# The low parts of the projection weights on GpSimd, with later due times in the order of TensorE's work

## The chip, the cores and the metric

One Trainium2 chip, one core of it. The metric is the device time of one execution in microseconds (us), the median over several runs. PE is TensorE, DVE is VectorE, ACT is ScalarE, POOL is GpSimd, SP is SyncE, whose queue starts most of the DMAs.

## The reference

One layer of a trunk with T = 1024 frames and width 1024, in float32. The input is normalised per frame and projected to many pieces; three gated recurrences (HGRN2 with 4 heads, GLA with 4 heads, mLSTM with 4 heads) work on the pieces in chunks of frames; their normalised and gated outputs are joined and projected back.

```python
h = _rmsnorm(x, norm_w[l])
parts = _split_columns(h @ w_in[l] + b_in[l])
y_hg = _gated_head_norm(_hgrn2_branch(parts, lower_bounds[l]), parts["hg_z"], hg_norm_w[l])
y_gla = _gated_head_norm(_gla_branch(parts, gla_w_a2[l], gla_b_a2[l]), parts["gla_z"], gla_norm_w[l])
y_ml = _gated_head_norm(_mlstm_branch(parts, ml_conv_w[l], ml_conv_b[l]), parts["ml_z"], ml_norm_w[l])
y = jnp.concatenate([y_hg, y_gla, y_ml], axis=-1).astype(x.dtype)
x = x + y @ w_out[l]
...
return _rmsnorm(x, final_norm_w)
```

## The kernel before

**Products.** Every float32 product of the projections is made of three matmuls on parts in the rounded type fp32r. A weight tile of 128x1024 goes through three steps in `load_w`: SP starts its DMA to `wraw` (two buffers), ACT copies it to the high part `whi` (rounding, line 230), and DVE subtracts to get the low part `wlo` (line 231). `whi` and `wlo` have four buffers each. PE then adds high x high, high x low and low x high in PSUM.

**Stages.** `proj_first` makes the first three pieces of head 0 (`f0`, `q0`, `z0`) while the input arrives, the weights cut into column parts (`cuts`). In it `row_sums` sums squares per frame, POOL raises the means to -1/2 (line 268), `row_scale` spreads the result over the partitions by transposes (line 275) and ACT copies it to `RSB` (line 276). The first pieces then leave PSUM through multiplications by `RSB` on DVE (line 339). The three wide loads (840, 840 and 560 columns, `load_wide`) are the weights of `v0`. After that `projections` runs over all other pieces: `proj_nt` (lines 346 to 348) and the transposed forms `proj_tn` and `proj_tn2` (lines 379 to 381 and 398 to 400), whose results DVE takes out of PSUM in `scaled` (line 406). The last part multiplies by the output weights in seven products of half size; the sums that these need are made by DVE in `sum_steps` (line 1075) along the way.

**The order of the work.** PE's order is set by the class `Weave`, at the time when the program is written: the projections are the main stream, and chains (trees, states, outputs, gates) are put between its matmuls. A chain yields its own cost on PE, a lag after which it may go on, and, if it holds a PSUM slot, for how long (`yield cost, lag, slot, hold`). These are estimates in model us (`proj_nt` counts 0.65 for three matmuls); the numbers decide after which projection matmul a chain's matmuls stand. In `proj_first` the orders of PE, ACT and SP are those of the code. All other orders, those of DVE and POOL among them, come from the scheduler of the framework, which keeps a fence `tc.issue_after(ins)`: what is issued in the block stands behind `ins` on the engine of `ins`.

**Chains that the change touches.** `radix4` (from line 440) is the finest step of the trees of the four HGRN2 heads; its `slack` is 1.2 for head 0 and 0 for the others. `tail` (line 655) makes a head's states and starts its outputs. `gla_alpha` (line 747) makes the gates of GLA: two rounds of logits in the PSUM slots `po` (line 750), a subtraction on DVE (line 768) that reads them, and an exponential on ACT. `ml_chain` makes the mLSTM heads: `ml_states` (line 851 on PE, line 857 on DVE, which writes the states `S`) and `ml_out` (lines 871 and 879 on PE, the latter reading `S`). `norm_transposed` normalises an output: squares on ACT (line 558), mean and power on POOL (lines 216 and 217), scaling on ACT (line 561), transposes on PE (line 566).

Of the kernel before, what the change touches and what calls it, by code (L numbers as in the profile page):

```python
# [7 lines left out]
F32 = mybir.dt.float32  # L8
F32R = mybir.dt.float32r
U8 = mybir.dt.uint8  # L10
AF = mybir.ActivationFunctionType
# [125 lines left out]
def kernel(ctx: ExitStack, tc: tile.TileContext, x, xt, wt, wide, cols, vbias, wa2, wq, fw, masks, sel,  # L137
                      ident_in, out):
    nc = tc.nc
# [9 lines left out]
    po = ctx.enter_context(tc.tile_pool(name="po", bufs=2, space=PS))  # L149
# [10 lines left out]
    RSB = const.tile([128, T], F32, name="RSB")  # L160
# [56 lines left out]
        nc.gpsimd.tensor_tensor(dst, dst, mhalf[:, 0:dst.shape[1]], op=OP.pow)  # L217


    def load_w(src, cuts=None, raw=None, hilo=None):  # L220

        raw = wp.tile([128, 1024], F32, name="wraw", bufs=2) if raw is None else raw
        if hilo is None:
            hilo = [wp.tile([128, 1024], F32R, name=nm, bufs=4) for nm in ("whi", "wlo")]
        hi, lo = hilo

        def part(a, b):
            s = slice(a, b)
            nc.sync.dma_start(raw[:, s], src[:, s])
            nc.scalar.activation(hi[:, s], raw[:, s], AF.Copy)  # L230
            nc.vector.tensor_sub(lo[:, s], raw[:, s], hi[:, s].bitcast(F32))  # L231
        if cuts is None:
            part(0, src.shape[1])
            return hi, lo
        return (hi, lo), [lambda a=a, b=b: part(a, b) for a, b in zip(cuts, cuts[1:])]

# [34 lines left out]
    def row_scale():  # L271
        for half in range(2):
            p = ptr.tile([128, 512], F32, name="tp")
            for j in range(4):
                nc.tensor.transpose(p[:, j * 128:(j + 1) * 128], rs[:, 4 * half + j:4 * half + j + 1].to_broadcast([128, 128]), ident)
            nc.scalar.activation(RSB[:, 512 * half:512 * half + 512], p, AF.Copy)


    wide_w, scales, marks = [], [], []
# [6 lines left out]
    def proj_first(pieces):  # L286

        ws, loads = [], []
        for i in range(3):
            raw = fp.tile([128, 1024], F32, name="al", bufs=2) if i == 2 else None  # L290
            t, steps = load_w(wt[WIDX[pieces[i][0]]], WCUTS, raw)
            ws.append(t)
            loads.append(steps)
        ps = [[pl.tile([128, 512], F32, name=nm) for _ in range(2)] for pl, nm in ((pmain, "pm"), (po, "po"), (ptree, "pt"))]
        done = [0, 0, 0]

        def matmuls(i, k):
            hi, lo = ws[i]
            for kk in range(done[i], k):
                ks = slice(128 * kk, 128 * kk + 128)  # L300
                for half in range(2):
                    s = slice(512 * half, 512 * half + 512)
                    nc.tensor.matmul(ps[i][half], hi[:, ks], HI[kk][:, s], start=kk == 0, stop=False)
                    nc.tensor.matmul(ps[i][half], lo[:, ks], HI[kk][:, s], start=False, stop=False)
                    nc.tensor.matmul(ps[i][half], hi[:, ks], LO[kk][:, s], start=False, stop=kk == KC - 1)
            done[i] = k
        for k in range(KC):
            if k == 0:
                loads[0][0]()
            build_h(k, 2 if k < 2 else 1)  # L310
            if k == 0:
                loads[1][0]()
                loads[2][0]()
            for i in range(3):
                for a in range(1, len(WCUTS) - 1):
                    if (WORDER[i] + 2 * (a - 1)) == k:
                        loads[i][a]()
            if k >= 3:
                square(k - 3)
            if k < KOUT:  # L320
                for i in range(3):
                    matmuls(i, k + 1)
        for k in range(KC - 3, KC):
            square(k)
        load_wide(0, [fp.tile([128, 1024], F32R, name="al", bufs=2) for _ in range(2)])
        matmuls(0, KC)
        load_wide(1)
        matmuls(1, SUMS)
        mean = row_sums()
        matmuls(1, KC)  # L330
        load_wide(2)
        matmuls(2, SCALE)
        row_scale()
        matmuls(2, KC)
        with tc.issue_after(mean):
            load_consts()
        for (_, dst, evac), pp in zip(pieces, ps):
            for half in range(2):
                nc.vector.tensor_mul(dst(half), pp[half], RSB[:, 512 * half:512 * half + 512])
                evac(half)  # L340

    def nt_half(hi, lo, s):
        p = pmain.tile([128, 512], F32, name="pm")
# [97 lines left out]
    def radix4(Q, K, F, Kc, dA, l4, slack):  # L441

        g = 4 ** l4
        n = 128 // g
        Q4, K4, F4 = (a.rearrange("p (n j g) -> p n j g", j=4, g=g) for a in (Q, K, F))
        P = [F4[:, :, j, g - 1:g] for j in range(4)]
        over = lambda j0, j1: F4[:, :, j0:j1, g - 1:g].to_broadcast([128, n, j1 - j0, g])
        qm = wk.tile([128, 768], F32, name="qm")  # L450
        M = qm.rearrange("p (n j g) -> p n j g", j=6, g=g)
        nc.scalar.activation(qm.rearrange("p (n x) -> p n x", n=n)[:, :, 0:3 * g],
                             Q.rearrange("p (n x) -> p n x", n=n)[:, :, g:4 * g], AF.Copy)
        nc.vector.tensor_tensor(M[:, :, 3:5, :], Q4[:, :, 2:4, :], over(1, 3), op=OP.mult)
        marks.append(nc.vector.tensor_tensor(M[:, :, 5, :], M[:, :, 4, :], P[1].to_broadcast([128, n, g]), op=OP.mult).ins)
        yield 0.0, 4.0 + slack
        yield "pt"
        p = ptree.tile([128, 512], F32, name="pt")
        for c in range(4):
            for a in range(0, 128, 32):  # L460
                q = (4 * c + a // 32) * 48
                nc.tensor.matmul(p[a:a + 32, 48 * c:48 * c + 48], Kc[:, c, a:a + 32], qm[:, q:q + 48], start=True, stop=True)
        pm = p[:, 0:192].rearrange("p (m j g) -> p m j g", j=6, g=g)
        d4 = dA.rearrange("p c (m j g) -> p (c m) j g", j=4, g=g)
        for off, j, w in ((0, 0, 3), (96, 3, 2), (160, 5, 1)):
            mask = mk4[:, l4, off:off + 32 * w].rearrange("p (m j g) -> p m j g", j=w, g=g)
            nc.vector.copy_predicated(d4[:, :, 4 - w:4, :], mask, pm[:, :, j:j + w, :])
        nc.vector.tensor_tensor(Q4[:, :, 1, :], Q4[:, :, 1, :], P[0].to_broadcast([128, n, g]), op=OP.mult)
        nc.vector.tensor_tensor(Q4[:, :, 2:4, :], M[:, :, 3:6:2, :], P[0][:, :, None].to_broadcast([128, n, 2, g]), op=OP.mult)
        nc.vector.tensor_tensor(P[2], P[2], P[3], op=OP.mult)  # L470
        nc.vector.tensor_tensor(P[1], P[1], P[2], op=OP.mult)
        nc.vector.tensor_tensor(K4[:, :, 0:3, :], K4[:, :, 0:3, :], over(1, 4), op=OP.mult)
        marks.append(nc.vector.tensor_tensor(P[3], P[0], P[1], op=OP.mult).ins)
        yield 0.7, 1.9 + slack, "pt", 3.0 + slack

    def tree(Q, K, F, A, dA, nh, half, done, slack=0.0):

# [171 lines left out]
    def tail(w, heads, rows, Q, K, F, V, zs, yi, trees, ready, out_done):  # L649

        yield lambda: ready() and 0 in trees
        S = wk.tile([128, NC, 130], F32, name="S", bufs=1)
        Kc = K.rearrange("p (c t) -> p c t", c=NC)
        states_done, first = [], []
        for half in range(2):
            yield lambda: half in trees
            yield from states(Kc, V[0], F, list(zip(heads, rows)), S, half)
            yield 0.0, 2.2
            states_done.append(half)
            if len(heads) > 1:  # L660
                w.start(pair_out(att, Q, V[0], S, zs, yi, half, states_done, first, out_done))
                continue
            for i, h in enumerate(heads):
                yield lambda: len(zs) > i
                w.start(att_out(h, att[:, (yi + i) % 2], Q[:, i], V[0], S, zs[i], yi + i, half, states_done, first, out_done))
# [77 lines left out]
    def gla_alpha(r, als):  # L743
# [21 lines left out]
        with tc.issue_after(marks[-1]):  # L765
            for half in range(2):
                s = slice(512 * half, 512 * half + 512)
                nc.vector.tensor_sub(al[:, s], ps[half], al[:, s])
        for half in range(2):
            yield 0.0, 0.0, "po", 2.0 + half  # L770
        nc.scalar.activation(al, al, AF.Exp, scale=1.0 / 16.0)
        als.append(al)

# [123 lines left out]
    def ml_chain(w, r, ready, PQK, Vs, ogs, gates, ys, zs, done):  # L897
# [22 lines left out]
        yield lambda: len(gates) == NC  # L920
        yield from ml_states(r, K, E, V, S, 1)
        states_of.append(r)
        yield from ml_out(r, Q, S, V, ogs[0], ys, 1, gates)
        for h in range(2):
            yield lambda: len(zs) > h
            for half in range(2):
                s = slice(512 * half, 512 * half + 512)
                dst = y_tile(4 + h)[:, 1] if r else ys[h]
# [263 lines left out]
    with tc.manual_schedule(engines={mybir.EngineType.PE}):  # L1192
# [87 lines left out]
        for c in range(4):  # L1280
            parts = [R] if c < 3 else [slice(512, 896), last]
            for n, cols in enumerate(parts):
                pc_ = slice(cols.start - 512, cols.stop - 512)
                p = ptree.tile([128, 512], F32, name="pt") if n else pa[c]
# [93 lines left out]
```

## Time and profile before

| what | value |
|---|---|
| median of 3 runs | 756.55 us (756.28 to 756.6) |
| the profiled execution, its own time | 757.12 us |
| its span in the trace | 755.3 us |
| busy: PE, DVE, ACT, POOL | 740.4, 471.6, 353.2, 60.2 us |

The span runs from the first to the last instruction in the trace; 1.8 us of the profiled execution lie outside it. Busy times count what an engine works on instructions; a matmul's weight load (PEld) overlaps the matmul before it. Rows of the trace have the start, the duration, the engine, the line of the code, the operation, the tiles and their sizes, and, in brackets, how long the engine stood idle before and whose end released it.

### The profile page before, as it was taken

The numbers are of one execution on the slowest core, as the hardware profiler recorded it, in microseconds if no ns is written. First come the engines' busy times: TensorE is split into PE (matmuls) and PEld (weight loads), VectorE is DVE, ScalarE is ACT, GpSimd is POOL, SyncE is SP. The second block draws the span as 40 slices with busy tenths as digits, with TensorE's granted clock in tenths as the row PEclk, the third lists the DMA queues.
The fourth block names the chain that finished last, engine by engine and source line by source line (L and its number), as shares of the span: only waits on it lengthen the run. The fifth ranks groups of instructions, "written<-read, shape, count | busy, mean of one in ns | idle before, by whom it ended". The sixth has DMA issues, their size and how long they took to land.

```text
span 755.3 us, 13831 instructions
## 1 busy us (share of the span) xinstructions
PE 740.4 (98%) x5550; PEld 619.6 (82%) x5550; DVE 471.6 (62%) x1004; ACT 353.2 (47%) x772; POOL 60.2 (8%) x107
## 2 busy tenths in 40 slices
PE   9999998999999999999999999999999999999996
PEld 7888886899887899788988878878877878888886
DVE  6987767766467538523662384353564358899864
ACT  6661577842343431544044553345270556454543
POOL 2000130010010020012001200101000110000011
PEclk9999999999999999999999999999999999999998
DMA  8443652332542232102020120031210077543323
GB/s 307 137 154 115 189 183 75 110 91 88 196 146 92 88 137 85 51 29 84 31 85 29 55 84 1 2 126 69 71 56 0 18 252 275 167 139 112 87 109 140
DMA packets 30545, 80.58 MB, mean 107 GB/s; under 512 B 3648, under 2 KB 7232, under 8 KB 30480
## 3 DMA queue, kind: packets, MB, share of 16 engines
q1 hardware_dynamic: 29664, 78.89, 31.3%
q8 instruction: 44, 0.72, 0.4%
q0 software_dynamic: 672, 0.53, 0.3%
q10 hardware_dynamic: 144, 0.26, 0.1%
q14 instruction: 21, 0.17, 0.1%
HBM read 63.74 MB, written 15.93 MB: 105 GB/s over the span
## 4 chain that ended last, share of the span: by engine, by line
PE 77%; ACT 7%; DVE 6%; DMA 6%; issue 1%; SPq 1%; POOL 0%; POOLq 0%; DVEq 0%; ACTq 0%
PE pm L346 10%; PE pm L348 10%; PE pm L347 9%; PE pm L398 4%; PE pm L379 4%; PE pm L400 4%; PE pm L399 4%; PE pm L380 3%; PE pm L381 3%; DMA wraw<-in_wt_dram 3%; DMA wraw<-in_wq_dram 2%; PE pm L1157 2%; PE pm L1158 2%; PE pm L1156 2%; DVE wlo L231 2%
## 5 line engine op out<-in xcount | busy, mean ns | idle before, releaser
L346 PE MATMUL pm<-hT,whi 128*128 128x512 f32 x400 | 163.5, 409 | 0.0
L348 PE MATMUL pm<-hT,wlo 128*128 128x512 f32 x400 | 156.8, 392 | 0.0
L347 PE MATMUL pm<-hT,whi 128*128 128x512 f32 x400 | 156.8, 392 | 0.0
L346 PEld LDWEIGHTS pm<-hT,whi 128*128 128x128 f32 x400 | 75.5, 189 | 16.9 <-issue 1.5
L348 PEld LDWEIGHTS pm<-hT,wlo 128*128 128x128 f32 x400 | 75.5, 189 | 16.7
L347 PEld LDWEIGHTS pm<-hT,whi 128*128 128x128 f32 x400 | 75.8, 189 | 13.6
L230 ACT ACTIVATE whi<-wraw 128x1024 fp32r<-128x1024 f32 (+4 forms) x47 | 45.7, 974 | 78.9 <-PE pm L347 31.7
L379 PE MATMUL pm<-whi,hT 128*128 128x256 f32 (+1 forms) x232 | 67.9, 293 | 0.0
L380 PE MATMUL pm<-wlo,hT 128*128 128x256 f32 (+1 forms) x232 | 66.0, 285 | 0.0
L381 PE MATMUL pm<-whi,hT 128*128 128x256 f32 (+1 forms) x232 | 66.0, 284 | 0.0
L231 DVE TENSOR_TENSOR wlo<-wraw,whi 128x1024 fp32r<-128x1024 f32 (+4 forms) x47 | 52.5, 1120 | 20.3 <-ACT whi L230 19.9
L406 DVE SCALAR_TENSOR_TENSOR big<-pm,rs,vb 128x256 f32<-128x256 f32 x72 | 30.9, 456 | 44.1 <-PE pm L400 27.3
L398 PE MATMUL pm<-whi,hT 128*128 128x512 f32 x128 | 52.5, 410 | 0.0
L400 PE MATMUL pm<-whi,hT 128*128 128x512 f32 x128 | 50.1, 392 | 0.0
L399 PE MATMUL pm<-wlo,hT 128*128 128x512 f32 x128 | 49.9, 390 | 0.0
L379 PEld LDWEIGHTS pm<-whi,hT 128*128 128x128 f32 x232 | 44.2, 190 | 0.8
L380 PEld LDWEIGHTS pm<-wlo,hT 128*128 128x128 f32 x232 | 44.3, 191 | 0.1
L381 PEld LDWEIGHTS pm<-whi,hT 128*128 128x128 f32 x232 | 44.2, 191 | 0.0
L533 ACT ACTIVATE att<-dc 32x128 f32<-32x128 f32 (+1 forms) x48 | 16.5, 343 | 54.8 <-DVE dc L513 54.3
L358 DVE TENSOR_TENSOR zg<-pm,RSB 128x512 f32<-128x512 f32 x22 | 15.2, 691 | 31.8 <-PE pm L348 26.7
L398 PEld LDWEIGHTS pm<-whi,hT 128*128 128x128 f32 x128 | 24.0, 188 | 7.7 <-issue 1.8
L400 PEld LDWEIGHTS pm<-whi,hT 128*128 128x128 f32 x128 | 24.0, 188 | 5.4
(391 smaller groups left out, 1502.4 us busy)
## 6 DMA issues: line engine op xcount, KB each, us to landing
wraw<-in_wt_dram SPq DMA_DIRECT2D x39, 512.0 KB, 3.8
wraw<-in_wq_dram SPq DMA_DIRECT2D x27, 512.0 KB, 3.6
wraw<-wsum SPq DMA_DIRECT2D x18, 512.0 KB, 3.5
wsum<-wraw SPq DMA_DIRECT2D x12, 512.0 KB, 2.9
big<-ydram SPq DMA_DIRECT2D x18, 256.0 KB, 5.4
ydram<-zg SPq DMA_DIRECT2D x8, 256.5 KB, 2.4
big<-in_xt_dram SPq DMA_DIRECT2D x4, 512.0 KB, 5.5
ydram<-zg SPq DMA_DIRECT2D x8, 255.5 KB, 2.6
```

The source lines that it names most:

```text
L230: nc.scalar.activation(hi[:, s], raw[:, s], AF.Copy)
L231: nc.vector.tensor_sub(lo[:, s], raw[:, s], hi[:, s].bitcast(F32))
L346: nc.tensor.matmul(p, hi[:, ks], HI[k][:, s], start=k == 0, stop=False)
L347: nc.tensor.matmul(p, hi[:, ks], LO[k][:, s], start=False, stop=False)
L348: nc.tensor.matmul(p, lo[:, ks], HI[k][:, s], start=False, stop=k == KC - 1)
L379: nc.tensor.matmul(p, HI[k][:, ts], hi[:, ks], start=k == 0, stop=False)
L380: nc.tensor.matmul(p, HI[k][:, ts], lo[:, ks], start=False, stop=False)
L381: nc.tensor.matmul(p, LO[k][:, ts], hi[:, ks], start=False, stop=k == KC - 1)
L398: nc.tensor.matmul(p, HI[k][:, ts], hi[:, ks], start=k == 0, stop=False)
L399: nc.tensor.matmul(p, HI[k][:, ts], lo[:, ks], start=False, stop=False)
L400: nc.tensor.matmul(p, LO[k][:, ts], hi[:, ks], start=False, stop=k == KC - 1)
L406: nc.vector.scalar_tensor_tensor(dst, p, rs[:, c:c + 1], b, op0=OP.mult, op1=OP.add)
```

## The change

The low part of a weight tile goes from DVE to POOL where the tile is loaded whole: 39 tiles of 128x1024 and the three wide ones. The cut tiles of `proj_first` and the tiles of the output product stay on DVE. The whole loads that follow `proj_first` are fenced behind ACT's second copy to `RSB` and behind the last multiplication of the evacuation (which is on DVE). Four due times in the order of PE's work are made later: radix4's lag and slot (by `slack`), the lag of `tail`, the slots of `gla_alpha`'s logits, and a new lag in `ml_chain` ahead of the second `ml_out`.

```diff
+    evacuated = []
...
-            nc.vector.tensor_sub(lo[:, s], raw[:, s], hi[:, s].bitcast(F32))
+            (nc.vector if cuts else nc.gpsimd).tensor_sub(lo[:, s], raw[:, s], hi[:, s].bitcast(F32))
         if cuts is None:
-            part(0, src.shape[1])
+            with ExitStack() as fences:
+                for ins in evacuated:
+                    fences.enter_context(tc.issue_after(ins))
+                part(0, src.shape[1])
...
-            nc.scalar.activation(RSB[:, 512 * half:512 * half + 512], p, AF.Copy)
+            copy = nc.scalar.activation(RSB[:, 512 * half:512 * half + 512], p, AF.Copy)
+        return copy.ins
...
-        row_scale()
+        scale = row_scale()
...
-                nc.vector.tensor_mul(dst(half), pp[half], RSB[:, 512 * half:512 * half + 512])
+                mul = nc.vector.tensor_mul(dst(half), pp[half], RSB[:, 512 * half:512 * half + 512])
                 evac(half)
+        evacuated.extend((scale, mul.ins))
...
-        yield 0.7, 1.9 + slack, "pt", 3.0 + slack
+        yield 0.7, 1.9 + 2.0 * slack, "pt", 3.0 + 2.0 * slack
...
-            yield 0.0, 2.2
+            yield 0.0, 3.2
             states_done.append(half)
...
-            yield 0.0, 0.0, "po", 2.0 + half
+            yield 0.0, 0.0, "po", 6.0 + half
...
         states_of.append(r)
+        yield 0.0, 3.5
         yield from ml_out(r, Q, S, V, ogs[0], ys, 1, gates)
```

After the change the lines below these places have numbers that are 2 to 8 higher (line 231 is 233, line 276 is 281, line 879 is 886).

ACT at the end of `proj_first`, before: the third wide tile, the first whole tile of the projections, then the copies to `RSB` and the sigmoid of `f0`.

```order
L230 ACTIVATE whi<-wraw 128x560
L230 ACTIVATE whi<-wraw 128x1024
L276 ACTIVATE RSB<-tp 128x512 x2
L950 ACT_TABLE_LOAD
L950 ACTIVATE f<-f,pc 128x512 x2
```

The same place with the change:

```order
L232 ACTIVATE whi<-wraw 128x560
L281 ACTIVATE RSB<-tp 128x512 x2
L232 ACTIVATE whi<-wraw 128x1024
L958 ACT_TABLE_LOAD
L958 ACTIVATE f<-f,pc 128x512 x2
```

The copies to `RSB` stand ahead of the first whole tile now.

POOL around the power of the row scale, before: the mask, the power, then copies for the gates.

```order
L175 AFFINE_SELECT neg<-neg 128x128
L268 TENSOR_TENSOR rs<-rs,mhalf 128x8
L432 COPY zg<-zg 128x1
L683 COPY big<-big 128x8x8
L685 COPY big<-big 128x8x16
```

With the change:

```order
L175 AFFINE_SELECT neg<-neg 128x128
L233 TENSOR_TENSOR al<-wraw,al 128x840
L233 TENSOR_TENSOR wlo<-wraw,whi 128x840
L273 TENSOR_TENSOR rs<-rs,mhalf 128x8
L233 TENSOR_TENSOR wlo<-wraw,whi 128x560
L233 TENSOR_TENSOR wlo<-wraw,whi 128x1024
L439 COPY zg<-zg 128x1
```

Two wide low parts stand ahead of the power, and one wide and the first whole one behind it.

PE in the second half of mLSTM (heads 0 and 1), before: the states, then at once the outputs, among projection matmuls.

```order
L348 MATMUL pm<-hT,wlo 128x512
L851 MATMUL pt<-big,kd 64x129 x6
L871 MATMUL po<-big,att 128x129 x4
L879 MATMUL po<-S,big 128x129 x4
L346 MATMUL pm<-hT,whi 128x512
```

With the change, the states:

```order
L858 MATMUL pt<-big,kd 64x129 x6
L353 MATMUL pm<-hT,whi 128x512
L354 MATMUL pm<-hT,whi 128x512
L355 MATMUL pm<-hT,wlo 128x512
```

and the outputs further on:

```order
L355 MATMUL pm<-hT,wlo 128x512
L878 MATMUL po<-big,att 128x129 x4
L886 MATMUL po<-S,big 128x129 x4
```

Between the two there are 18 projection matmuls now; before there were none.

## Rows read from the trace of the kernel before

**Rows 1.** The page: busy time, share of the span and instructions of each engine.

```profile
PE 740.4 (98%) x5550; PEld 619.6 (82%) x5550; DVE 471.6 (62%) x1004; ACT 353.2 (47%) x772; POOL 60.2 (8%) x107
```

**Rows 2.** PE's waits: who waited, for whom; us in all, how often, the longest.

```profile
PE po L879 <- DVE S L857: 2.2, 2, 1.2
PE po L750 <- DVE al L768: 1.6, 1, 1.6
PE pm L379 <- DVE f L339: 1.5, 1, 1.5
...
PE pm L379 <- DVE big L406: 0.9, 2, 0.7
PE pt L462 <- DVE f L470: 0.5, 1, 0.5
PE pt L592 <- ACT kd L575: 0.4, 1, 0.4
PE po L640 <- DVE S L598: 0.4, 1, 0.4
```

**Rows 3.** Timeline of the first evacuation: start us, us, engine, line, operation.

```profile
40.93 1.06 ACT L276 ACTIVATE RSB<-tp 128x512 f32<-128x512 f32 x2
...
41.06 1.22 DVE L231 TENSOR_TENSOR wlo<-wraw,whi 128x1024 fp32r<-128x1024 f32 x1 [1.66 <-ACT whi L230]
...
42.20 0.68 DVE L339 TENSOR_TENSOR f<-pm,RSB 128x512 f32<-128x512 f32 x1
...
42.94 0.40 PE L379 MATMUL pm<-al,hT 128*128 128x280 f32 x1 [1.53 <-DVE f L339]
```

**Rows 4.** Window after L750's wait: busy PE, PEld, DVE, ACT, POOL, granted clock, DMA.

```profile
126.00:131.00 5.00, 5.00 (x45) 3.89 (x46) 2.33 (x9) 4.90 (x10) 0.00 (x0) 0.66 0.01 3
```

**Rows 5.** Groups by line and shape: busy us, mean ns, then idle before.

```profile
L231 DVE TENSOR_TENSOR wlo<-wraw,whi 128x1024 fp32r<-128x1024 f32 x39 | 47.7, 1226 | 19.9 <-ACT whi L230 19.5
...
L685 POOL COPY big<-big 128x128 f32<-128x128 f32 x1 | 0.4, 435 | 0.0
...
L683 POOL COPY big<-big 128x64 f32<-128x64 f32 x1 | 0.3, 307 | 23.6 <-DVE big L406 23.6
```

**Rows 6.** Timeline of the row scale.

```profile
31.85 1.03 DVE L231 TENSOR_TENSOR al<-wraw,al 128x840 fp32r<-128x840 f32 x1 [0.20 <-DVE big L247]
...
35.32 1.68 POOL L268 TENSOR_TENSOR rs<-rs,mhalf 128x8 f32<-128x8 f32 x1 [29.57 <-DVE rs L267]
...
37.63 1.04 PE L275 MATMUL tp<-ident,rs 128*128 128x128 f32 x8
```

**Rows 7.** Timeline of a low part with little time to its first use.

```profile
495.79 2.59 DVE L231 TENSOR_TENSOR wlo<-wraw,whi 128x1024 fp32r<-128x1024 f32 x2 [1.60 <-ACT whi L230]
...
499.26 0.19 PEld L348 LDWEIGHTS pm<-hT,wlo 128*128 128x128 f32 x1
```

**Rows 8.** Timeline of a tree step with a low part inside.

```profile
296.96 1.22 DVE L231 TENSOR_TENSOR wlo<-wraw,whi 128x1024 fp32r<-128x1024 f32 x1
...
298.09 0.28 DVE L530 TENSOR_TENSOR al<-al 128x64 f32<-128x64 f32 x1
...
299.07 0.43 PE L491 MATMUL pt<-big,f 128*32 128x32 f32 x28
```

**Rows 9.** Timeline of an mLSTM norm: scaling, then transposes.

```profile
515.02 1.26 ACT L561 ACTIVATE osb<-osb,st 128x128 f32<-128x128 f32 x4
...
518.97 0.60 PE L566 MATMUL tp<-ident,osb 128*128 128x128 f32 x4
```

**Rows 10.** Timeline of DVE and POOL at work at the same time, two places.

```profile
3.40 1.83 POOL L173 MEMSET att<- 128x2048 f32 x1
...
4.35 1.06 DVE L208 TENSOR_SCALAR lb<-lb 128x4 f32<-128x4 f32 x1
...
102.54 1.23 DVE L1075 TENSOR_TENSOR wraw<-wraw 128x1024 f32<-128x1024 f32 x1 [2.64 <-DMA wraw<-in_wq_dram]
...
102.92 0.89 POOL L216 TENSOR_SCALAR st<-st 128x4 f32<-128x4 f32 x1
```

## The prediction

> **What bounds the kernel now.** I read the page first: PE is busy for 740.4 us, 98% of the span, DVE for 62%, ACT for 47%, POOL for 8% [rows 1]. PE is the bound and the change takes no matmul away, so all it can win is time in which PE stands or runs slowly, and all it can lose is new time of that kind. Freeing DVE is worth nothing in itself.
>
> PE's waits are read next [rows 2]. Beside the start of the program, which the change doesn't touch, there are seven groups: 2.2 + 1.6 + 1.5 + 0.9 + 0.5 + 0.4 + 0.4 = 7.5 us. Six of the seven are waits for DVE, and no one waits for a low part. The reader is to see that they are few and single: each has its own place.
>
> The granted clock gives one more term. In the 5 us that begin after the 1.6 us wait of L750, PE is busy all the time at a granted clock of 0.66 [rows 4], a mean over the two levels of 1.2 and 2.4 GHz: 5 x 0.34 = 1.7 us lost. So L750 costs 1.6 + 1.7 = 3.3 us, and all that can be won is 7.5 + 1.7 = 9.2 us.
>
> **The change part by part.** The sum is made against the profiled execution, 757.12 us (span 755.3 and 1.8 outside it); it lies 0.57 above the median, 756.55, so 0.57 comes off at the end.
>
> *First evacuation.* PE waits 1.5 us for `f` [rows 3]. DVE starts on it at 42.20, when its low part (41.06, 1.22 us) is done, and `RSB` was copied from 40.93 on, behind a whole tile's copy on ACT. The changed order puts the copies to `RSB` ahead of that tile, and the low part is on another engine: either alone moves the start by about 1 us, and both by more than 1.5. I take -1.5. The fence on the multiplication holds no DVE instruction any more, since the fenced block issues on SP, ACT and POOL; only the fence on the copy acts.
>
> *Logits of GLA.* PE waits at L750 for `al`, since the PSUM slot was counted free too early; the order now has the next user 4 model us later. That covers the 1.6 us wait, and with it the slow stretch: -1.6 - 1.7 = -3.3. The main stream's matmuls fill the place, so the later slot costs PE nothing; without such matmuls it would move the stall to another place.
>
> *Tail and mLSTM.* `tail` gets 1.0 us more ahead of L640, which waits 0.4: -0.4. In mLSTM 18 projection matmuls now stand between states and outputs; the program counts three at 0.65 us, so 3.9 us, well over the two waits at L879, 2.2 in all [rows 2]: -2.2. The norm behind them is later by the same 4 us; it ends in the main stream, which has matmuls left.
>
> *Radix4.* Only head 0 has slack, and no wait of [rows 2] lies on it as it is; 0, covered by the projections of `v0`.
>
> So waits with a remedy: 1.5 + 3.3 + 0.4 + 2.2 = 7.4. The others (0.9 + 0.5 + 0.4 = 1.8) have none of their own; they wait for DVE or ACT, and DVE has 47.7 us less to do [rows 5]. I take half: -0.9, between 0 and -1.8.
>
> *The low parts on POOL.* No row shows a two-input POOL operation on 1024 columns. Its copies of 64 and 128 columns took 307 and 435 ns [rows 5]: 2.0 ns a column, so 307 + 960 x 2.0 = 2.2 us for 1024 columns with one input. The lower end is DVE's own 1.23 us; the upper one is 4.4 us, twice the copy, if the two inputs are read one after the other. I take 2.2, the row nearest in engine and kind. On these rows 42 low parts give POOL some 90 us more, against 60 busy now: it has room on the average. The Trainium skill (GPSIMD Engine Reference, § Performance versus the Vector engine) has 4497 ns on GpSimd for an addition of 2048 columns, so an estimate of 2.2 us for 1024; the sum by it would be the same.
>
> Does PE then wait for a low part? The tightest that I found is the first of two in a row; it begins at 495.79 and is used at 499.26 [rows 7]. At 2.2 us it is ready at 498.0, in time; at 4.4 us at 500.2, 0.9 late. Most others are ready far ahead, since there are four buffers. With two such places that is 0 to 2 us, and I take 0.
>
> *The row scale.* Two wide low parts now stand ahead of the power. DVE made them from 31.85; on POOL each takes 0.82 x 2.2 = 1.8 us, so until about 35.4, where the power starts already (35.32, 1.68 us); the transposes follow at 37.63, 0.6 us after its end [rows 6]. That holds at 2.2 us and costs 3 us at 4.4 (2 x 3.6 from 31.85 is 39.1, and PE would stand until 40.8). I take 0.
>
> *Trees.* Of the 39 low parts [rows 5], 14 fall into tree steps by the timeline. In the one shown [rows 8] DVE made a low part until 298.18, the step's last product ended at 298.37, and PE's next matmul came at 299.07: 0.7 us of slack. If POOL's low part leaves DVE alone, the step is 1.2 us earlier and PE gains nothing; if it holds DVE's operands up for all its 2.2 us, PE waits 2.2 - 0.7 = 1.5. Between 0 and 1.5 each I take 0.1, near the lower end since most steps have 1 to 2 us of slack: +1.4.
>
> *Norms.* In the second half of mLSTM the power stands in POOL's queue behind low parts, in the change's order. The scaling ends at 516.28, 2.7 us ahead of the transposes at 518.97 [rows 9]. One low part ahead fits in; two of 2.2 us cost 1.7. Between 0 and 1.7 I take +0.5.
>
> *Places that move.* All later work of PE's order is shifted by the new due times, and DVE's by the missing low parts; where a slot is met early, a wait of the size of those in [rows 2] (0.4 to 1.6 us) arises. I take +0.9, one of middle size.
>
> Sum: 757.1 - 7.4 - 0.9 + 1.4 + 0.5 + 0.9 = 751.6; less 0.57: **751.0 us**.
>
> **The rivals.** *All gone, nothing new:* 757.1 - 9.2 - 0.57 = 747.3. For it: the remedies hit the places of [rows 2] one by one. Against it: each shift of PE's order opens others.
>
> *Gain given back:* POOL's order mixes low parts with the powers and the small copies of the gates, and what stood idle is late now. With 3 to 6 us of such waits in addition (two clock drops as in [rows 4] suffice) it ends at 753 to 758.
>
> *DVE pays for POOL's reads, the rival on the slow side.* POOL's clear of `att` ran from 3.40 to 5.23; DVE's operation on 4 columns, begun at 4.35, took 1.06 us and ended just after it, where 64 columns take 0.28 [rows 8, 10]. The other way round, a POOL operation on 4 columns took 0.89 us, beginning inside an addition of DVE and ending with it [rows 10]. So one engine can hold the other up for the whole of an instruction. The Trainium skill (SBUF — State Buffer, § Who interferes with whom) has the rule: the second DVE port pair is shared with GpSimd as an exclusive lock, and a DVE instruction with two SBUF inputs blocks with a GpSimd one that reads SBUF, whoever issues first. The trace agrees in the second pair; the first, one input beside a clear, is not that case, and shows a hold all the same. The place is the trees, whose DVE steps are products of two SBUF tiles: each of the 14 low parts in them stops DVE for its whole length. Against the 1.23 us of DVE that it spares and the common slack of 1.5 us, that costs (length - 2.7) x 14. At 2.2 us nothing, at 3.45 us 10.5, which eats the 9.2 and makes it 1.3 slower; beyond about 3.5 us it decides. At 3.7 us: 747.3 + 14 = 761; at 4.4 us: 747.3 + 23.8 = 771. Since the two hold each other up in turn, POOL's low parts are lengthened by DVE too, which speaks for it; that POOL's copies go at 2.0 ns a column speaks against.
>
> *It doesn't do what it says:* the low parts are moved for certain; of the remedies only the fence on `RSB` might not bite, and then 1.5 comes back: 752.5, inside the forecast's own range.
>
> **How the numbers follow.** What a measurement of this kernel can tell from no change is about 0.2%, 1.5 us: 755.0 to 758.1. The forecast's own range, 748.9 to 753, holds the bounds of the trees, the norms and the moved places taken one at a time; 0.51. All gone 0.15. Given back 0.16, of which 0.04 is faster, 0.11 same, 0.01 slower. DVE pays 0.18, of which 0.17 is slower and 0.01 same. So faster 0.51 + 0.15 + 0.04 = 0.70, same 0.12, slower 0.18. The range reaches from 747.0 to 759.0: it leaves out the most of the slow rival and a sliver below 747.
>
> **What would show it.** Right: no wait of PE at L757 (now 750), no 0.66 window after it, none at L886 (now 879), the first L386 within 0.3 us of its predecessor; low parts on POOL of 2 to 2.5 us in the groups by line; PE's waits together below 4 us. Wrong: low parts above 3.5 us; DVE steps of the trees, 0.3 us now, at 2 us or more beside a POOL row; PE waiting for `wlo`, for `rs` at the row scale, or for `osb` behind POOL's powers. Any wait of over a microsecond followed by a granted clock under 1.0 would weigh twice.

## The result: slower by 3%, in three lumps

The changed kernel takes 779.60 us (778.93 to 779.88) where the kernel before takes 756.55; the ratio is 1.0304, with an interval of 1.0281 to 1.0327. The forecast was 751.0, within 747 to 759. The page of the changed kernel says where the 23 us are not: engine times against [rows 1] are DVE 8 us less and POOL 118 us more, and PE 7 us more for the same matmuls.

```profile
PE 747.1 (96%) x5550; PEld 623.0 (80%) x5550; DVE 463.2 (60%) x962; ACT 353.0 (45%) x772; POOL 177.8 (23%) x149
```

DVE was to lose 47.7 us of whole low parts and some 3 us of wide ones; it is only 8 us less busy, so its other operations take over 40 us more. The groups by line and shape show where, for instance in the trees. Kernel before:

```profile
L528 DVE TENSOR_TENSOR big<-big,f 128x256 f32<-128x256 f32 x24 | 10.1, 419 | 5.6 <-PE pt L522 5.6
...
L529 DVE TENSOR_TENSOR f<-f,al 128x256 f32<-128x256 f32 x28 | 11.7, 417 | 0.0
```

The same two groups with the change, and POOL's low parts:

```profile
L536 DVE TENSOR_TENSOR f<-f,al 128x256 f32<-128x256 f32 x28 | 16.1, 573 | 0.0
...
L535 DVE TENSOR_TENSOR big<-big,f 128x256 f32<-128x256 f32 x24 | 14.8, 618 | 5.9 <-PE pt L529 5.7
```

```profile
L233 POOL TENSOR_TENSOR wlo<-wraw,whi 128x1024 fp32r<-128x1024 f32 x39 | 96.6, 2483 | 275.2 <-ACT whi L232 251.3 <-issue 23.8
...
L439 POOL COPY zg<-zg 128x1 f32<-128x1 f32 x12 | 18.3, 1527 | 16.7 <-ACT zg L437 16.6
```

Two things are odd. Means of tree steps rise by a third to a half though only a few of each group meet a low part, and a copy of one column takes 1.5 us in the mean of twelve. Counted by single rows, DVE has 15 operations of 2 us or more now; before it had none.

PE's waits, in the columns of [rows 2]:

```profile
PE po L1164 <- ACT whi L1115: 6.2, 1, 6.2
PE po L621 <- DVE S L605: 3.7, 2, 3.2
PE tp L696 <- POOL big L690: 2.8, 1, 2.8
PE pt L498 <- DVE dc L474: 2.2, 1, 2.2
...
PE po L757 <- ACT osb L568: 1.3, 1, 1.3
PE pm L386 <- DVE big L413: 1.3, 2, 1.0
PE pt L498 <- DVE f L536: 1.0, 2, 0.7
PE pt L469 <- DVE f L477: 0.8, 1, 0.8
```

The wait for the first `f`, the two at L879 (now L886), the one for `al` at L750 (now L757) and that at L640 (now L647) are gone. The remedies hit their places. But leaving out the wait at the start of the program, the waits sum to 22.8 us where they were 7.5, and three of them are over 2.5 us. Behind these three PE runs slowly. Each of the three waits, together with the slow stretch behind it, is called a lump below. Windows of the changed kernel (the number after the five engines is the granted clock):

```profile
72.00:81.00 9.00, 6.09 (x42) 4.59 (x30) 6.34 (x13) 5.97 (x14) 4.89 (x6) 0.62 0.39 125
107.00:112.00 5.00, 4.59 (x22) 4.25 (x23) 1.57 (x2) 2.03 (x12) 2.09 (x2) 0.66 0.37 144
...
666.00:678.00 12.00, 5.86 (x13) 4.30 (x14) 6.34 (x9) 5.09 (x7) 0.00 (x0) 0.57 0.49 151
```

So each has its price twice, as L750 had in [rows 4]. Counting slow time only while PE is busy after the wait (2.8, 1.7 and 2.9 us), the three lumps are 5.6, 4.9 and, with a 0.5 us wait right behind, 9.7 us: 20.2 us. The span has grown by 22.5 us, and two figures make up 22.0 of it: all waits together are 15.3 us longer (22.8 less 7.5), and PE is busy 6.7 us longer with the same matmuls. The second price is not always due: behind the 2.2 us wait at L498 the clock stays at 1.00 here.

**The first two lumps** are the same picture. Timeline, changed kernel:

```profile
72.21 2.34 POOL L233 TENSOR_TENSOR wlo<-wraw,whi 128x1024 fp32r<-128x1024 f32 x1 [11.97 <-ACT whi L232]
...
72.42 2.41 DVE L535 TENSOR_TENSOR big<-big,f 128x256 f32<-128x256 f32 x1
...
74.50 0.50 POOL L690 COPY big<-big 128x64 f32<-128x64 f32 x1
...
75.05 0.42 PE L696 MATMUL tp<-ident,big 128*64 128x128 f32 x1 [2.85 <-POOL big L690]
...
102.88 3.05 DVE L475 TENSOR_TENSOR big<-big,f 128x128 f32<-128x128 f32 x1
...
103.31 2.36 POOL L233 TENSOR_TENSOR wlo<-wraw,whi 128x1024 fp32r<-128x1024 f32 x1
...
107.41 0.38 PE L621 MATMUL po<-S,big 128*1 128x128 f32 x2 [3.25 <-DVE S L605]
```

A DVE step of 0.4 us takes 2.4 or 3.0 us and ends within 0.3 us of the end of the low part beside it. At 72 us the small copy for the gates stands behind the low part in POOL's queue, and PE waits for it. At 103 us the states `S` stand behind the held step in DVE's queue.

**The third lump** has no low part in it. Timeline of several engines:

```profile
648.80 14.38 POOL L439 COPY zg<-zg 128x1 f32<-128x1 f32 x1 [7.55 <-ACT zg L437]
...
663.21 0.80 SPq L1213 DMA_DIRECT2D zg<-in_x_dram  x2
664.11 0.38 SPq L1114 DMA_DIRECT2D wraw<-in_wq_dram  x1
...
670.51 1.06 ACT L1115 ACTIVATE whi<-wraw 128x1024 fp32r<-128x1024 f32 x1 [10.08 <-DMA wraw<-in_wq_dram]
...
671.62 0.79 PE L1164 MATMUL po<-whi,hT 128*128 128x512 f32 x1 [6.24 <-ACT whi L1115]
```

POOL's copy of one column of the last gate `zg` lasts 14.38 us. Meanwhile DVE runs products and differences of two SBUF tiles, one after the other without a gap, from 647.5 to 663.1 us; the copy ends when DVE stops. The tile's next use is a load that stands in SP's queue; behind it stands the load of an output weight, and PE waits for that weight. In the kernel before, the same copy took 0.49 us:

```profile
636.95 0.49 POOL L432 COPY zg<-zg 128x1 f32<-128x1 f32 x1 [11.72 <-ACT zg L430]
```

### The profile page after: what moved, and what is told of

Its sections match the earlier page's. It is cut to its first block, busy times and chain, and to the rows that moved or that the text cites. A ratio compares the mean times of both kernels' runs of the same rounds, so it can differ in the third digit from the quotient of the medians.

```text
span 777.8 us, 13818 instructions
## 1 busy us (share of the span) xinstructions
PE 747.1 (96%) x5550; PEld 623.0 (80%) x5550; DVE 463.2 (60%) x962; ACT 353.0 (45%) x772; POOL 177.8 (23%) x149
## 4 chain that ended last, share of the span: by engine, by line
PE 47%; POOL 2%; ACT 2%; DVE 2%; DMA 1%; issue 1%; SPq 0%; POOLq 0%; DVEq 0%; ACTq 0%
PE pm L353 5%; PE pm L354 5%; PE pm L355 5%; PE pm L405 4%; PE pm L407 4%; PE pm L406 4%; POOL zg L439 2%; PE pm L386 1%; PE po L1165 1%; PE tp L1165 1%; PE tp L1164 1%; PE pt L1165 1%; PE pt L1164 1%; PE tp L1166 1%; PE pt L1166 1%; PE po L1166 1%
## 5 line engine op out<-in xcount | busy, mean ns | idle before, releaser
L233 POOL TENSOR_TENSOR wlo<-wraw,whi 128x1024 fp32r<-128x1024 f32 (+2 forms) x41 | 100.0, 2444 | 275.2 <-ACT whi L232 251.3
L386 PE MATMUL pm<-whi,hT 128*128 128x256 f32 (+1 forms) x232 | 67.8, 292 | 0.0
L386 PEld LDWEIGHTS pm<-whi,hT 128*128 128x128 f32 x232 | 44.2, 191 | 0.8
L388 PEld LDWEIGHTS pm<-whi,hT 128*128 128x128 f32 x232 | 44.3, 191 | 0.0
L216 POOL TENSOR_SCALAR st<-st 128x4 f32<-128x4 f32 x24 | 7.3, 302 | 132.0 <-ACT sq L565 131.4
L565 ACT ACTIVATE sq<-po 128x128 f32<-128x128 f32 x64 | 17.7, 276 | 33.4 <-PE po L647 14.2
```

Source lines behind the costliest of these rows:

```text
L233: (nc.vector if cuts else nc.gpsimd).tensor_sub(lo[:, s], raw[:, s], hi[:, s].bitcast(F32))
L386: nc.tensor.matmul(p, HI[k][:, ts], hi[:, ks], start=k == 0, stop=False)
L388: nc.tensor.matmul(p, LO[k][:, ts], hi[:, ks], start=False, stop=k == KC - 1)
```

## Experiments

Two theories at the start. A: POOL's low parts and DVE's two-input operations hold each other up. B: the later due times moved PE's order for the worse. Each run is compared with runs of the kernel before on the same chip.

### All low parts back on DVE (lows_dve)

```diff
-            (nc.vector if cuts else nc.gpsimd).tensor_sub(lo[:, s], raw[:, s], hi[:, s].bitcast(F32))
+            nc.vector.tensor_sub(lo[:, s], raw[:, s], hi[:, s].bitcast(F32))
```

> The changed kernel with all low parts back on DVE, so the remedies alone. Theory A (POOL's low parts and DVE's two-input operations hold each other up at SBUF, and that makes the loss): without POOL's low parts the three large waits (2.8 us at L696, 3.3 at L621, 6.2 at L1164) and the slow stretches behind them are gone; 748 to 756 us. Theory B (the later due times themselves moved PE's order so that it waits): the loss stays, 770 to 780 us.

766.54 us, ratio 1.0134 (1.0118 to 1.0151): neither. The lump at L696 is gone; L621 still waits 2.3 us, and the copy of `zg` lasts 14.38 us again, with 5.9 us at L1164. So the remedies carry a loss of their own, and the starved copy needs no low part on POOL. The wait at L621 needs none either: how much of its 3.2 us in the changed kernel is due to the held step is not shown.

### The low parts alone (pool_only)

The opposite: the kernel before with that one line of the change and no remedy.

> The kernel before with only the whole low parts moved to POOL, without fences and later due times. Theory A: DVE's tree steps beside a low part of 2.5 us take 2 us or more, some 20 times; 765 to 785 us. Theory B: POOL has room, so within 2 us of the kernel before, 755 to 759 us.

777.14 us (775.41 and 778.87), ratio 1.0276: the time of theory A. DVE has 12 operations of 2 us or more, where the expectation had some 20. The copy of `zg` takes 0.49 us here. The largest waits:

```profile
PE po L871 <- DVE osb L886: 5.3, 2, 3.1
PE po L750 <- ACT osb L561: 3.9, 2, 2.9
PE po L614 <- DVE S L598: 1.7, 1, 1.7
```

### The one-column copy on ACT (halo_act)

```diff
-                nc.gpsimd.tensor_copy(z[:, 0:1], z[:, T:T + 1])
+                nc.scalar.activation(z[:, 0:1], z[:, T:T + 1], AF.Copy)
```

> The changed kernel with the one-column copy of zg (L439) on ACT. Theory A: that copy took 14.4 us on POOL, since DVE's two-input operations ran without a gap, and SP's queue behind it started a weight DMA late; without it the 6.2 us wait at L1164 and the slow stretch behind it go, 768 to 771 us. Rival: the weight DMA is late for its raw buffer and not for that copy, then 778 to 780 us.

770.10 us (768.83 and 771.37), ratio 1.0182: as expected, and no wait is left at L1164. The one-column copy cost 9.2 us (1.0304 less 1.0182, times 756.5). This is a net figure, since other places moved too: L621 waits only 0.6 us at the most here, where the step ahead of it is done before the low part begins, and the wait of 2.2 us at L498, which cost no clock in the changed kernel, is followed here by a slow stretch until 140 us. Two pairs of runs give the copy 7.3 us (lows_dve less remedies_halo) and 9.5 us (halo_pool less fence_ml).

### Low parts in four pieces (low_quarters)

```diff
+            n = (b - a) if cuts else 256
+            for q in range(a, b, n):
+                t = slice(q, min(q + n, b))
+                (nc.vector if cuts else nc.gpsimd).tensor_sub(lo[:, t], raw[:, t], hi[:, t].bitcast(F32))
```

> The changed kernel with each whole low part as four POOL instructions of 256 columns. Theory A (a hold lasts as long as one POOL instruction): DVE's held operations shorten from 2.4 to below 1 us, the waits at L621 and L696 shrink by half or more, 765 to 775 us. Rival C (POOL is late by its total work and its queue, not by single holds): POOL's work grows by the fixed cost of three more instructions a tile, 780 to 788 us.

778.62 us, ratio 1.0295: the time lies between the two expectations. Single holds are shorter, as theory A had it, and only one of the two waits shrank. In the timeline at the place of the second lump (lines are 3 higher here):

```profile
101.94 3.44 POOL L236 TENSOR_TENSOR wlo<-wraw,whi 128x256 fp32r<-128x256 f32 x4 [3.11 <-ACT whi L232]
...
102.25 0.80 DVE L481 TENSOR_TENSOR f<-f 128x128 f32<-128x128 f32 x1
...
103.23 0.68 DVE L478 TENSOR_TENSOR big<-big,f 128x128 f32<-128x128 f32 x1
103.82 1.00 DVE L479 TENSOR_TENSOR big<-qm,f 128x256 f32<-128x256 f32 x1
```

No step is held for more than about a piece of POOL's work, but now several in a row are, in turn with POOL, and POOL's four pieces take 3.44 us in place of 2.4. The wait at L621 (here L624) falls from 3.2 to 1.8 us; that at L696 (here L699) rises from 2.8 to 3.7, where the gate's copy stands behind low parts in POOL's queue. The starved copy, 14.39 us, is in this run as well. Cutting the work up spread the hold and won nothing in time.

### The remedies without the starved copy (remedies_halo)

The edits of lows_dve and halo_act together.

> All remedies of the change, low parts on DVE, and the one-column copy of zg on ACT. If the remedies alone were 10 us slower only because that copy was starved (5.9 us wait, 0.5 behind it and some 3 us of slow clock), 756 to 758 us: the remedies then win nothing in sum, since waits at L580, L621 and L498 came in their place. Rival: the copy was not the cause, 765 to 768 us.

758.04 us, ratio 1.0037 (1.0021 to 1.0054): as expected, at the upper edge. The remedies alone bring nothing in sum. Their largest wait is a new one:

```profile
PE po L621 <- DVE S L605: 2.1, 1, 2.1
```

Between this run and halo_act lie the low parts on POOL alone: 1.0182 less 1.0037, times 756.5, is 11.0 us. The two traces say how it is paid. Engine times of remedies_halo, then of halo_act:

```profile
PE 740.0 (98%) x5550; PEld 618.1 (82%) x5550; DVE 470.7 (62%) x1004; ACT 357.9 (47%) x786; POOL 59.1 (8%) x95
```

```profile
PE 746.0 (97%) x5550; PEld 622.1 (81%) x5550; DVE 460.0 (60%) x962; ACT 355.0 (46%) x784; POOL 158.4 (21%) x137
```

PE is busy 6.0 us longer with the same matmuls, in two slow stretches; remedies_halo has none between 20 and 740 us. PE's waits are 4.8 us longer. So the larger part of the price is the clock.

### Two remedies, then three, then four (fence_ml, fence_ml_po, fence_ml_po_tail)

From remedies_halo, radix4's slack, the lag of `tail` and the slots of the logits are put back; what stays is the fence and the mLSTM lag.

```diff
-        yield 0.7, 1.9 + 2.0 * slack, "pt", 3.0 + 2.0 * slack
+        yield 0.7, 1.9 + slack, "pt", 3.0 + slack
...
-            yield 0.0, 3.2
+            yield 0.0, 2.2
...
-            yield 0.0, 0.0, "po", 6.0 + half
+            yield 0.0, 0.0, "po", 2.0 + half
```

> Low parts on DVE, copy of zg on ACT, and of the remedies only the two that leave the first 130 us of PE's order alone but for the fence: the fence behind RSB and the lag of 3.5 in mLSTM. If these two remove their waits (1.5 and 2.2 us) and nothing new comes, 752 to 754 us. Rival: the earlier evacuation opens the waits of 86 to 131 us by itself, 756 to 758 us.

753.03 us, ratio 0.9961 (0.9948 to 0.9974): 3.0 us faster by the ratio, as expected, with the copy of `zg` on ACT. Then the slots of the logits are 6.0 again:

> As the run with fence and mLSTM lag, with the later slots of GLA's logits in addition. If these remove the wait at L757 and its slow stretch (3.3 us): 749 to 751 us. Rival: the held slots push the first head's outputs back, so that L621 waits for S by 2 us or more and its slow stretch follows: 755 to 758 us.

753.96 us, ratio 0.9973 (0.9964 to 0.9983): between the two cases, and no gain over fence_ml. The wait at L757 and its slow stretch are gone, but in their place PE waits 2.1 us at L580 and 1.7 us at L498 in the trees, a slow stretch behind the first of these, and not at L621 as the rival had it. Then the lag of `tail` as well:

> The run with fence, mLSTM lag and GLA slots (754.0 us) with the lag of tail at 3.2 in addition. All remedies together took 758.0 us, with a wait of 2.1 us at L621 for the states. If the later lag of tail makes that wait: 756 to 758 us. Rival: radix4's doubled slack for head 0 makes it: 753 to 755 us.

754.52 us, ratio 0.9980 (0.9969 to 0.9991): the rival. No wait at L621. What is left between this and remedies_halo is radix4's doubled slack for head 0: 1.0037 less 0.9980, times 756.5, is 4.3 us, by difference; it was not run by itself.

### The gates' small copies on ACT too (small_act)

The changed kernel with the edit of halo_act and the copies L690 and L692 on ACT, the first of them in two parts.

> The changed kernel, low parts on POOL, with the copy of zg and the two copies for the gates (L690, L692) on ACT. The copies stood behind a low part in POOL's queue, and PE waited 2.8 us at L696 with 2.6 us of slow clock behind it. Theory A: without them 764 to 766 us; the rest over the kernel before stays with DVE's held tree steps (L498). Rival: PE waits at L696 as long for the held DVE step ahead (L535), 769 to 771 us.

768.04 us, ratio 1.0161: two us below halo_act, not the five of theory A, and neither case of the expectation. L696 waits no more; others do:

```profile
PE pt L469 <- DVE f L477: 3.1, 1, 3.1
PE po L757 <- ACT osb L568: 2.9, 1, 2.9
```

Each of the two is followed by a slow stretch. A lump that is taken out at one place comes up at the next place that lacks slack.

### Which low parts (early_pool, late_pool)

From fence_ml, the engine of the low part by the piece's name, here and at the other whole loads: mLSTM's names begin with m.

```diff
-        hi, lo = load_w(wt[WIDX[name]])
+        hi, lo = load_w(wt[WIDX[name]], low=nc.gpsimd if name[0] != 'm' else nc.vector)
```

> The run with fence and mLSTM lag (753.0 us), with the low parts of the HGRN2 and GLA pieces (23 tiles, among them those that fall into tree steps) on POOL, those of mLSTM and the wide ones on DVE. Theory A (what costs are low parts beside DVE's chains of two-input steps that PE waits for): 763 to 768 us, with waits for DVE at the trees and slow stretches behind them. Rival: any low part on POOL costs its share, 23 of 39, so 760 us.

763.59 us, ratio 1.0099: against fence_ml 10.4 us more (0.0138 times 756.5). The time is as expected, the place only in part: the largest wait, 3.4 us in two, is at L757 for `osb`, and not at the trees.

> The same with the low parts of the mLSTM pieces alone (16 tiles) on POOL. Theory A: there DVE has slack and the lag covers the outputs, so 752 to 755 us. Rival: the share of 16 of 39 of some 12 us, 758 us; its place would be L878, which waited 5.3 us for DVE where all low parts were on POOL and there was no lag.

754.90 us, ratio 0.9987 (0.9977 to 0.9998): 2.0 us more for 16 tiles, as expected. Together 12.4 us, against 11.0 for all of them in the change. It is not the number of tiles that counts: 23 early ones cost 10.4 us, 16 late ones 2.0. Nor is it the number of holds: DVE has five operations of 2 us or more in either run. In early_pool a slow stretch follows the wait at L757; late_pool has none.

### POOL at work, but not reading (early_write)

```diff
+            if low is nc.gpsimd:
+                low.tensor_copy(lo[:, s][:, 0:1], hi[:, s][:, 0:1].bitcast(F32))
+                for n in (1024, 1024, 512):
+                    low.memset(lo[:, 0:n].bitcast(F32), 0.0)
+            nc.vector.tensor_sub(lo[:, s], raw[:, s], hi[:, s].bitcast(F32))
```

> As the run with the 23 early low parts on POOL (763.6 us), but the low parts are made by DVE, and POOL has in the place of each a one-column copy of the high part and three clears of the low tile (2560 columns in all, about 2.5 us) that only write and that DVE's subtraction then overwrites. If POOL's reads of SBUF hold DVE up and make most of the loss: DVE's steps beside the clears keep their usual 0.3 to 0.7 us, 753 to 757 us. If it is POOL's queue (the powers of the norms stand behind a piece of work of 2.5 us): the waits at L757 for osb stay, 760 to 765 us.

757.07 us, ratio 1.0012 (0.9999 to 1.0026): the first case, at its upper edge. Timeline of POOL and DVE (lines are 4 higher; L539 is L535 of the change):

```profile
73.58 2.55 POOL L236 MEMSET wlo<- 128x1024 f32 x3
...
73.75 0.42 DVE L540 TENSOR_TENSOR big<-big,f 128x256 f32<-128x256 f32 x1
74.08 0.42 DVE L539 TENSOR_TENSOR big<-big,f 128x256 f32<-128x256 f32 x1
74.42 0.42 DVE L540 TENSOR_TENSOR big<-big,f 128x256 f32<-128x256 f32 x1
```

Beside 2.55 us of clears, the steps keep the 0.42 us that the groups of the kernel before show; beside a low part of 2.34 us one took 2.41. In the whole run no DVE operation takes 2 us. It is POOL's reads that hold DVE's two-input operations. By the ratios 6.6 of the 10.4 us are gone; whether the reads alone made them is not shown, since the low parts are back on DVE here and the scheduler placed the powers of the norms otherwise. What is left over fence_ml has with it a wait of 2.7 us at L473 for DVE (in early_pool, as L469, it is 0.2), whose cause was not traced. That the queue has a share is seen in early_pool:

```profile
100.92 2.40 POOL L233 TENSOR_TENSOR wlo<-wraw,whi 128x1024 fp32r<-128x1024 f32 x1 [1.45 <-ACT whi L232]
...
106.35 2.05 POOL L217 TENSOR_TENSOR st<-st,mhalf 128x4 f32<-128x4 f32 x2
...
111.61 1.12 ACT L568 ACTIVATE osb<-po,st 128x128 f32<-128x128 f32 x4
...
112.79 0.80 PE L757 MATMUL po<-RX,wa 96*128 96x512 f32 x1 [2.71 <-ACT osb L568]
```

The same power in fence_ml:

```profile
97.59 1.05 POOL L217 TENSOR_TENSOR st<-st,mhalf 128x4 f32<-128x4 f32 x1
```

In early_pool it comes at 106.35, behind the low part and behind DMA work of POOL. ACT's scaling came to stand behind a later activation, and PE waited 2.71 us for its slot. POOL's queue makes about 4 of the 8.8 us between the two; the squares ahead of the power were 4.7 us later already.

The Trainium skill (SBUF — State Buffer, § Who interferes with whom) says that a DVE instruction with two SBUF inputs contends with a GpSimd instruction that reads SBUF and not with one that only writes it. The two timelines, 2.41 us beside a low part and 0.42 us beside clears, agree.

### What makes the copy starve (halo_pool)

fence_ml with the copy of `zg` on POOL again, as in the kernel before.

> The run with fence and mLSTM lag, with the copy of zg back on POOL, as in the kernel before. If the lag in mLSTM (which shifts the last outputs against the output product's first steps on DVE) is what lets that copy fall into DVE's run without gaps: the copy takes over 10 us, and 760 to 763 us. Rival: it takes the low parts or the other due times for that, then 753 us as with the copy on ACT.

762.68 us, ratio 1.0087: as expected.

```profile
632.33 14.39 POOL L439 COPY zg<-zg 128x1 f32<-128x1 f32 x1 [7.55 <-ACT zg L437]
```

So one of the two edits that are left in fence_ml makes the copy starve. The fence acts 590 us earlier, and the lag moves just these outputs, so by its place it is the lag; this is argued and not shown, since neither was run by itself. Why the copy got in after 0.49 us in the kernel before, where DVE was about as dense, was not seen.

### A smaller step for the logits (po_three)

```diff
-            yield 0.0, 0.0, "po", 2.0 + half
+            yield 0.0, 0.0, "po", 3.0 + half
```

> The run with fence and mLSTM lag, with the slots of GLA's logits held for 3.0 + half model us in place of 2.0 (the change has 6.0). If 1 us is enough for L757's wait of 1.5 us and leaves the trees' order nearly as it was: 750 to 752 us. Rival: as with 6.0, another place waits instead, 753 to 755 us.

752.31 us, ratio 0.9951 (0.9934 to 0.9968): the fastest of all, though not told apart from fence_ml, and just above the first case. As the rival had it, another place waits: the wait at L757 has gone to L498. But no slow stretch follows it: the clock is 1.00 from 118 to 130 us.

```profile
PE pt L498 <- DVE dc L474: 1.7, 1, 1.7
...
PE pm L386 <- DVE big L413: 1.2, 2, 0.8
```

## Why the prediction was wrong

Three terms of the sum failed. Trees and norms stood at 1.4 and 0.5 us for all that the low parts on POOL would cost; they cost 11.0 us. The places that move stood at 0.9 us; the starved copy alone cost 9.2 us. The radix4 slack stood at 0 and cost 4.3 us, by difference.

The change by its parts, as differences of ratios times 756.5 us, each uncertain by 1 to 2 us:

| part | us | from |
|---|---|---|
| fence and mLSTM lag | -3.0 | fence_ml |
| GLA slots | +0.9 | fence_ml_po |
| lag of tail | +0.5 | fence_ml_po_tail |
| radix4's slack | +4.3 | remedies_halo |
| low parts on POOL | +11.0 | halo_act |
| the starved copy of zg | +9.2 | the changed kernel |
| sum | +22.9 | |

The parts add up because each run is one step from its neighbour; in another order they are other numbers. Put into the kernel before, the low parts alone cost 20.9 us (pool_only). With them there, the remedies win 7.1 us (halo_act less pool_only), where without them they lose 2.8 us (remedies_halo).

*First evacuation, -1.5:* right. The start of L345 moved from 42.20 [rows 3] to 39.42, and PE doesn't wait for `f`.

*Logits, -3.3:* the wait and its slow stretch went, as the step had it; but "the later slot costs PE nothing" failed. Other waits took its place (L580, L498 with low parts on DVE), and the sum of this part is +0.9, not told from 0. With 3.0 in place of 6.0, po_three is no worse than without.

*Tail and mLSTM, -2.6:* right for the waits. "The norm behind them is later by the same 4 us; it ends in the main stream" looked no further than PE. By its place it is this lag that makes the last gate's copy starve (halo_pool); by what steps was not traced.

*Radix4, 0:* "covered by the projections of v0" was wrong by 4.3 us. The 2.1 us wait for states at L621 comes with it; how the slack leads to that wait was not traced, and the 4.3 us are a difference between two runs, since the slack was not run by itself.

*The other waits, -0.9:* not seen. In the changed kernel L386 waits 1.3 us for `big` (0.9 before) and L469 0.8 us for `f` (0.5 before).

*Low parts on POOL, 2.2 us each:* 2.48 in the mean, 2.34 to 2.4 undisturbed; the copies' slope was a good guide, and PE waits for none of these low parts. The row scale was right as well: two low parts of 2.00 us, the power at 35.55, the transposes at 37.36, no wait.

*Trees, +1.4, and norms, +0.5:* the step that failed. Together with the queue they cost 11.0 us. The forecast took 0.1 us a tree step, near the lower end of 0 to 1.5, "since most steps have 1 to 2 us of slack"; the one step that it shows has 0.7, and no row shows the others. Three things are missing in that working: a step is held to the end of POOL's instruction, and everything behind it in DVE's queue as well; POOL's small work (gate copies, powers) stands behind the low part too; and a wait of 2 to 3 us can be paid twice, in the wait and in the slow stretch behind it, which made 6.0 of the 11 us. The last one was in the text for L750, and was not applied to new waits. Nor does the range "hold the bounds of the trees": 14 steps at 1.5 us are 21 us, which ends far above 753.

*The rival on the slow side* had the mechanism and its place, and the wrong price: "at 2.2 us nothing", and a point of decision at 3.5 us. At 2.48 us it already cost more than all the waits that were to be won. A threshold with one average slack for 14 steps can't see that a few steps carry the loss. So the sign that it gave, low parts above 3.5 us, was no sign; the other, tree steps of 2 us or more beside a POOL row, came.

*Places that move, +0.9:* by far too little. The starved copy alone is 9.2 us. Its signs stood in the trace before: a POOL operation of 4 columns held until DVE's end [rows 10], and DVE busy without a gap at the start of the output product. What wasn't asked is which POOL work is due there, and who waits behind it. That it would starve in the changed order and not in the order before could not be told from these rows.

## What to carry to other kernels

Before work goes to POOL, look for DVE's chains of operations on two SBUF tiles beside it: while POOL's low parts read SBUF here, each held the other for whole instructions, and cutting POOL's work up only spread the hold. The price is not the mean but the two or three places without slack, where a wait is paid once as a wait and, in most of these lumps, again as a slow clock. When a due time is moved, follow the moved work to its end, and ask what small operation on POOL, and what load in SP's queue, is due there.

## What the runs showed of the hardware that was not expected

A POOL copy of one column can be kept waiting 14.4 us by DVE operations on two SBUF tiles that follow each other without a gap: not for one instruction, but until DVE stops. In the trace of before, the POOL operation at [rows 10] was held for 0.89 us, until the DVE instruction beside it ended. The copy of the last gate took 14.4 us in the change, in lows_dve, in low_quarters and in halo_pool, and as an ACT copy it held nothing up. It need not come so: in the kernel before and in pool_only the same copy took 0.49 us.

DVE operations with one SBUF input can be held too. A product and sum on 1024 columns in mLSTM takes 0.81 us in the kernel before and 2.38 us beside a low part of 2.40 us; the means of the two before and with the change:

```profile
L800 DVE TENSOR_SCALAR al<-f,pc 128x1024 f32<-128x1024 f32 x2 | 1.6, 808 | 0.0
...
L807 DVE TENSOR_SCALAR al<-f,pc 128x1024 f32<-128x1024 f32 x2 | 4.8, 2378 | 1.6 <-ACT f L817 1.6
```

For such operations clears are not free either: one on 512 columns took 1.16 us beside the clears of early_write, where the eight of the kernel before take 0.54 us in the mean.
